# Rotary embedding on one core: the loads of slabs 5 to 7 and the stores of slabs 0 to 3 go in runs of 4 KB instead of 32 KB

## The chip, the cores and the metric

The kernel runs on one core of a Trainium2 chip. The metric is device time in microseconds (us), the median of several executions; lower is better. The profile is of one execution. Its engines are ScalarE (ACT), VectorE (DVE), GpSimd (POOL), TensorE (PE) and SyncE (SP), and there are 16 DMA engines that move data between HBM and SBUF for all queues.

## The reference

A rotary position embedding over x of 16 batches x 512 positions x 1024 values (float32, 33.55 MB), seen as 16 heads of 64. Within a head the two halves of 32 are turned by the angle of the position:

```python
x = x.reshape(batch, seq, num_heads, head_dim)
x1, x2 = x[..., :half_dim], x[..., half_dim:]
cos = cos[None, :, None, :]
sin = sin[None, :, None, :]
rotated = np.concatenate([x1 * cos - x2 * sin,
                          x1 * sin + x2 * cos], axis=-1)
```

cos and sin are 512 x 32 float32 tables (64 KB each). The output has the shape and type of x, so 33.55 MB are read and 33.55 MB written.

## The kernel before

**Tiling.** The 16 batches are worked through as 8 slabs of two batches each (`nb = 2`). A slab is 128 partitions x 8192 float32 values, so 32 KB in each partition and 4 MB in all. One partition holds 8 consecutive positions of 1024 values (`rpp = 8`), which are contiguous in HBM and in SBUF. `dram(t, s)` on L47 describes a slab in HBM as 128 rows of `W` = 8192 contiguous elements. A load or a store of a slab is one DMA of 128 runs of 32 KB, 8 runs for each of the 16 DMA engines.

**Slots.** Five slabs have room in SBUF (`slots = 5`). Slabs 0 to 4 are loaded at once at the start. Slab s + 5 takes the place of slab s, so `load(s + 5)` waits until the store of slab s has landed in HBM. The call stands behind the store in the program, on L143.

**Queues.** SyncE issues the loads of slabs 0 to 5 and the two small loads of cos and sin (which follow the load of slab 0). GpSimd issues the loads of slabs 6 and 7. ACT issues all eight stores, between its own compute instructions. On the profile's page q1 is SyncE's DMA queue, q10 is ACT's and q0 is GpSimd's.

**Tables.** POOL casts cos and sin to bf16, PE spreads them over the 128 partitions with a selection matrix, and DVE copies them to `tab` once. This is over before the first slab is worked on.

**Work on a slab.** A slab is worked on in passes: slabs 1 to 5 in one pass of 8192 elements per partition, slabs 0, 6 and 7 in two passes of 4096. For each pass ACT casts the float32 slab to bf16 (`xb`, L112), DVE does two multiplications (L133) and one addition (L136), and ACT casts the result back to float32 into the slab itself (L139). After the last pass of a slab ACT issues its store (L141). Two buffers `xb` alternate.

**Order.** The order on each engine is the program's order; nothing is planned at run time. ACT's order is: cast of the next pass, copy-out of this pass, then, if the slab is complete, its store. The cast of the first half of slab 7 therefore stands ahead of the copy-out of the second half of slab 6 and ahead of the store of slab 6. If slab 7 has not landed, ACT waits there.

## Time and profile before

| what | value |
|---|---|
| median of 3 runs | 162.8 us (162.47 to 166.78) |
| span of the profiled execution | 160.2 us |
| ACT busy | 113.5 us (71%), 23 instructions |
| DVE busy | 108.6 us (68%), 34 instructions |
| bytes moved by DMA | 67.24 MB, mean 420 GB/s |
| load of a slab from SyncE, issue to landing | 26.6 us (median) |
| load of a slab from GpSimd, issue to landing | 24.9 us (median) |
| store of a slab from ACT, issue to landing | 25.9 us (median) |

The profiled execution's own time is not given apart from its span, from its first to its last instruction. The median of the runs is 2.6 us above that span; this difference holds what lies around the instructions, and what one execution differs from another.

In the page, a row of digits cuts the span in 40 equal slices of 4 us; each digit is the busy share in tenths, 9 being 90% or more. A DMA queue's row has its packets, its megabytes, and the time that its packets took as a share of 16 engines. The shares of all queues together say how full the DMA engines were. A row of a group of instructions has the line, the engine, the operation, out <- in with the shapes and the count, then the total busy time, the mean of one in ns, and behind the last bar the idle time of the engine just before them with what ended it. A timeline row has the start and the duration in us. "ACTq", "SPq" and "POOL ... DMA_DIRECT2D" rows are issues of DMAs, not the transfers.

### The profile page before, as it was taken

Reading aid. Unit: us, or ns where it says so; the run is one execution under the profiler, and the core shown is the slowest. Engines: PE = TensorE matmul, PEld = TensorE weight load, DVE = VectorE, ACT = ScalarE, POOL = GpSimd, SP = SyncE. Lnnn points to the kernel's source line nnn. Section 1 sums busy time; section 2 is a strip of 40 time slices with the busy share of each in tenths; the row PEclk is TensorE's granted clock in tenths of the full one; section 3 lists DMA queues with packets and bytes.
Section 4 is the critical chain, followed back from the end, with each engine's and each line's share of the span. In section 5 each row is a group of like instructions: output and inputs, shape, how many; then the busy total and the mean of one; then the engine's idle time right before and its main releaser. Section 6 shows DMA issues by size and latency. Waiting matters only on the chain.

```text
span 160.2 us, 159 instructions
## 1 busy us (share of the span) xinstructions
PE 1.0 (1%) x4; PEld 0.5 (0%) x4; DVE 108.6 (68%) x34; ACT 113.5 (71%) x23; POOL 3.0 (2%) x11
## 2 busy tenths in 40 slices
PE   0002000000000000000000000000000000000000
PEld 0000000000000000000000000000000000000000
DVE  0001899999979979997997299919839499940000
ACT  3006929998999999899919995089995999553000
POOL 2001000000000000000010001000000000000000
DMA  7999999999999999999999999999999999999995
GB/s 246 409 393 426 393 450 466 393 417 491 401 393 426 491 393 409 499 401 393 483 434 393 450 466 393 426 483 401 409 491 409 393 475 442 393 442 475 393 426 229
DMA packets 2464, 67.24 MB, mean 420 GB/s; under 512 B 288, under 2 KB 416, under 8 KB 416
## 3 DMA queue, kind: packets, MB, share of 16 engines
q10 hardware_dynamic: 1152, 33.55, 48.5%
q1 hardware_dynamic: 1024, 25.30, 37.5%
q0 software_dynamic: 288, 8.39, 12.1%
HBM read 33.69 MB, written 33.55 MB: 420 GB/s over the span
## 4 chain that ended last, share of the span: by engine, by line
DMA 49%; ACT 28%; issue 8%; DVE 4%; SPq 1%; ACTq 0%; POOLq 0%
DMA slab<-in_x_dram 29%; DMA out_dram<-slab 20%; ACT slab L139 16%; ACT xb L112 12%; DVE xb L136 1%; DVE xb L133 1%; DVE slab L133 1%; SPq L73 1%; ACTq L141 0%; SPq L64 0%; POOLq L174 0%; ACTq L139 0%; POOLq L64 0%
## 5 line engine op out<-in xcount | busy, mean ns | idle before, releaser
L112 ACT CAST xb<-slab 128x4096 bf16<-128x4096 f32 (+1 forms) x11 | 56.6, 5155 | 27.8 <-DMA slab<-in_x_dram 26.5
L139 ACT CAST slab<-xb 128x4096 f32<-128x4096 bf16 (+1 forms) x11 | 56.6, 5154 | 3.5 <-DVE xb L136 3.5
L133 DVE TENSOR_TENSOR slab<-xb,tab 128x4096 bf16<-128x4096 bf16 (+1 forms) x11 | 35.9, 3260 | 17.3 <-ACT xb L112 17.2
L133 DVE TENSOR_TENSOR xb<-xb,tab 128x4096 bf16<-128x4096 bf16 (+1 forms) x11 | 35.9, 3261 | 0.3
L136 DVE TENSOR_TENSOR xb<-xb,slab 128x4096 bf16<-128x4096 bf16 (+1 forms) x11 | 35.9, 3261 | 0.3
L103 DVE CAST tab<-acc 128x1024 bf16<-128x1024 f32 x1 | 1.2, 1225 | 15.2 <-PE acc L97 15.2
L64 POOL DMA_DIRECT2D slab<-in_x_dram x2 | 1.2, 608 | 84.1 <-DMA out_dram<-slab 84.1
L112 ACT ACT_TABLE_LOAD x1 | 1.3, 1283 | 0.7 <-PEq L160 0.7
L97 PE MATMUL acc<-tab,pick 64*128 64x256 bf16 x4 | 1.0, 402 | 14.2 <-POOL tab L92 14.2
L92 POOL CAST tab<-cos_sb 64x256 bf16<-64x256 f32 x1 | 0.4, 389 | 12.1 <-DMA cos_sb<-in_cos_dram 12.1
L85 POOL TENSOR_SCALAR_AFFINE_SELECT pick<-pick 64x128 bf16<-64x128 bf16 x2 | 0.5, 285 | 0.1
L97 PEld LDWEIGHTS <-pick 64*128 64x128 bf16 x4 | 0.5, 122 | 14.2 <-issue 12.6
L92 POOL CAST tab<-sin_sb 64x256 bf16<-64x256 f32 x1 | 0.4, 394 | 0.0
L82 POOL MEMSET pick<- 64x256 bf16 x1 | 0.3, 304 | 0.3 <-POOLq L160 0.3
L160 POOL MEMSET const-float32-0.0<- 128x1 f32 x1 | 0.1, 103 | 0.2 <-issue 0.2
L160 POOL MEMSET const-bfloat16-1.0<- 128x1 bf16 x1 | 0.1, 107 | 0.0
L160 POOL MEMSET const-uint8-127<- 128x1 uint8 x1 | 0.1, 106 | 0.0
L160 POOL MEMSET const-float32-1.0<- 128x1 f32 x1 | 0.1, 103 | 0.0
## 6 DMA issues: line engine op xcount, KB each, us to landing
out_dram<-slab ACTq DMA_DIRECT2D x8, 4096.0 KB, 25.9
slab<-in_x_dram SPq DMA_DIRECT2D x6, 4096.0 KB, 26.6
slab<-in_x_dram POOLq DMA_DIRECT2D x2, 4096.0 KB, 24.9
cos_sb<-in_cos_dram SPq DMA_DIRECT2D x1, 64.0 KB, 12.5
sin_sb<-in_sin_dram SPq DMA_DIRECT2D x1, 64.0 KB, 12.3
```

The source lines that it names most:

```text
L64: queue.dma_start(out=slab[s], in_=dram(x, s))
L73: nc.sync.dma_start(out=t, in_=bass.AP(tensor=src.tensor, offset=src.offset, ap=[[TW, SP], [1, TW]]))
L82: nc.gpsimd.memset(pick, 0.0)
L85: nc.gpsimd.affine_select(out=part, in_=part, compare_op=mybir.AluOpType.not_equal, fill=1.0 - 2.0 * g, base=0, pattern=[[0, P // SP], [-1 ...
L92: nc.gpsimd.tensor_copy(out=view(tab1, i * TW, (1, TW)), in_=t)
L97: nc.tensor.matmul(view(acc, i * rpp * hd + h * half, (hd, rpp), (1, half)), view(pick, i * h * P, (1, P)), view(tab1, i * TW, (half, rpp) ...
L103: nc.vector.tensor_copy(out=tab, in_=acc)
L112: nc.scalar.copy(out=view(xb[s], r * dim, (1, n * dim)), in_=view(slab[s], r * dim, (1, n * dim)))
L133: nc.vector.tensor_mul(out=t, in0=xu, in1=view(tab, a + r * hd, (hd, n), (0, nh), (1, hd)))
L136: nc.vector.tensor_add(out=xu, in0=xu, in1=view(t2, half, (hd, n * nh), (-half, 2), (1, half)))
L139: nc.scalar.copy(out=xs, in_=xu)
L160: nc = _bacc.Bacc("TRN2", target_bir_lowering=False, num_devices=1)
```

## The change

A keyword `max_dma_last_dim` (in bytes) limits the length of one run of a DMA. With `4 * W` it is the whole row of a slab, 32 KB, as before; with `4 * dim` it is 4 KB, so that each of the 128 rows is cut in 8 runs and the DMA has 1024 runs.

- The loads of slabs 0 to 4 keep runs of 32 KB; those of slabs 5, 6 and 7 go in runs of 4 KB.
- The stores of slabs 0 to 3 go in runs of 4 KB; those of slabs 4 to 7 keep 32 KB.
- The loads of slabs 6 and 7 are issued by SyncE instead of GpSimd, so all loads are in SyncE's queue.

Compute, bytes, slots, waits and the order on ACT and DVE stay as they are.

```diff
     def load(s):
 
-        queue = nc.sync if s < nslabs - 2 else nc.gpsimd
         slab[s] = slabs.tile([P, W], f32, tag="slab", name="slab")
-        queue.dma_start(out=slab[s], in_=dram(x, s))
+        nc.sync.dma_start(out=slab[s], in_=dram(x, s),
+                          max_dma_last_dim=4 * (W if s < slots else dim))
 
...
 
         nc.scalar.copy(out=xs, in_=xu)
         if r + n == rpp:
-            nc.scalar.dma_start(out=dram(out_flat, s), in_=slab[s])
+            nc.scalar.dma_start(out=dram(out_flat, s), in_=slab[s],
+                                max_dma_last_dim=4 * (dim if s < 4 else W))
             if s + slots < nslabs:
                 load(s + slots)
```

## The prediction

> **What bounds the kernel now.** I read the page's second and third parts first, then the chain, then the groups, and last the DMA queues in short windows. From the page:

> ```profile
> DMA  7999999999999999999999999999999999999995
> DMA packets 2464, 67.24 MB, mean 420 GB/s; under 512 B 288, under 2 KB 416, under 8 KB 416
> q10 hardware_dynamic: 1152, 33.55, 48.5%
> q1 hardware_dynamic: 1024, 25.30, 37.5%
> q0 software_dynamic: 288, 8.39, 12.1%
> DMA 49%; ACT 28%; issue 8%; DVE 4%; SPq 1%; ACTq 0%; POOLq 0%
> L112 ACT CAST xb<-slab 128x4096 bf16<-128x4096 f32 (+1 forms) x11 | 56.6, 5155 | 27.8 <-DMA slab<-in_x_dram 26.5
> ```

> The DMA engines are busy in all 40 slices; the three queues' shares add to 98.1% of the span (157.2 of 160.2 us). ACT, the busiest compute engine, works 113.5 us and waits 26.5 us for loads. So the bytes are the bound: no reordering alone can gain more than the 3.0 us in which the engines are not all busy, and of those 1.7 us precede the first packet and 1.2 us follow the last. The packet records give 1213 ns for a 32 KB packet in the mixed stages, started every 1209.5 ns, so one slab is 8 x 1.2095 = 9.68 us of every engine.

> How do loads and stores share the engines? Three windows of 1.2 us, one packet time each, show it. The columns of a queue row are packets, MB and share of 16 engines. First 65.0 to 66.2 us:

> ```profile
> q1 hardware_dynamic: 16, 0.52, 101.1%
> ```

> Then 66.2 to 67.4 us:

> ```profile
> q10 hardware_dynamic: 16, 0.52, 101.1%
> ```

> Then 67.4 to 68.6 us:

> ```profile
> q1 hardware_dynamic: 16, 0.52, 101.1%
> ```

> Each window holds 16 packets, one per engine, of one queue only: SyncE's loads (q1), ACT's stores (q10), loads again. **The queues take turns of one 32 KB packet.** Equal halves of the bandwidth are thus a consequence of equal packets. The change makes the packets unequal.

> The end hangs on slab 7. From the timeline:

> ```profile
> 99.23 0.53 POOL L64 DMA_DIRECT2D slab<-in_x_dram  x1 [18.65 <-DMA out_dram<-slab]
> ...
> 124.22 3.60 ACT L112 CAST xb<-slab 128x4096 bf16<-128x4096 f32 x1 [1.85 <-DMA slab<-in_x_dram]
> ...
> 131.37 0.34 ACTq L141 DMA_DIRECT2D out_dram<-slab  x1
> ...
> 145.54 0.34 ACTq L141 DMA_DIRECT2D out_dram<-slab  x1
> ```

> Load 7 lands at T = 124.22. ACT takes its first half ahead of slab 6's second copy-out (program order), so store 6 is issued at T + 7.15 and store 7 at T + 21.32. Store 6's last packets end at 149.1, so store 7, issued at 145.54, finds the engines still fed: a margin of 3.6 us, less about 1.0 us from an issue to a first packet (slab 0: issued at 0.74, first packet at 1.74).

> **The parts of the change.**

> *Descriptor overhead.* Seven of the sixteen transfers (stores 0 to 3, loads 5 to 7) go in 4 KB packets: 64 instead of 8 per engine and slab. No 4 KB packet is in the trace; bound it by the 1 KB packets of cos and sin (46 ns long, started 42 ns apart) and the 32 KB ones. A line through the starts gives 155 ns for 4 KB, through the durations 159 ns. Eight of them are 1240 to 1272 ns against 1210 or 1213: 30 to 59 ns more per 32 KB. With 7 x 8 = 56 such runs per engine that is 1.7 to 3.3 us of pure engine time, nothing beside which it could hide. Below zero is excluded, since a 32 KB packet already runs at 27.0 GB/s per engine and smaller ones only add starts. I take 156 ns, near the starts (they are what a queue can deliver): 9.98 us per slab, +2.2 us in all.

> *Issue.* One ACT issue of 128 rows took 338 ns, SyncE's 328 to 585, the 64-row cos and sin 522 and 583: no growth with rows is seen. If it grew with packets, 8 x 338 = 2.7 us, so 2.4 us more on ACT for each of four stores, 9.5 us before its cast of slab 5 at 84.2. Its waits there (3.54 us at 84.2, 6.69 at 104.8) swallow that. I take zero. If ACT were even held at each issue until the store before had drained, store 4 would be issued near 113 and store 5 near 124, still before step 4 below needs them.

> *SyncE instead of GpSimd for loads 6 and 7.* It removes two GpSimd issues (0.69 and 0.53 us) and puts two behind load 5 on SyncE, which has nothing else to do by then. Load 7 already started only behind load 6. Worth: zero.

> *Turns of unequal length.* This decides. Step by step, T of load 7 after the change:

> 1. Loads 3 and 4 (32 KB) beat store 0 (4 KB) 8 to 1 and land earlier. ACT is busy then (22.8 of 23.6 us from 37.6 to 61.2), so nothing is won. Loads 0 to 4 and store 0 together were served by 62.0 us; with 8 x 0.04 us more, store 0's data now ends at 62.3.
> 2. Load 5 waits for its landing. Before, it was 0.45 us to the issue and 4.4 us (61.21 to 65.6) to the first packet, two queued 32 KB packets (2.4 us) among it. Two 4 KB packets instead are 0.3 us: store 1 has the engines alone for 2.7 us (bounds 1.5, from slab 0's 1.0 us, and 4.8, as before).
> 3. Then loads 5, 6, 7 and stores 1, 2, 3 alternate, 4 KB each, and the stores stay 2.7 us of service ahead. Store 3 ends at 62.3 + 2.7 + 2 x (3 x 9.98 - 2.7) = 119.5. Load 7 was issued at about 100, behind load 6, and has 2.7 / 0.156 = 17 packets per engine left.
> 4. From here ACT's queue holds stores 4 and 5 (issued near 98 and 116) in 32 KB packets. A turn of both queues costs 1.21 + 0.156 = 1.366 us and moves one 4 KB packet of load 7. Before, the same turn moved 32 KB. Stores 4 and 5 have 16 packets, so 16 turns, 21.9 us, to 141.4; the last packet and 0.45 us to the landing: **T = 141.9**.
> 5. Store 6 can't be issued until T + 7.15 = 149.1. Queue and engines are empty from 141.5, which is new idle time.
> 6. The end: T + 21.3 (store 7's issue) + 1.2 (first packet) + 9.7 (its 8 packets alone) + 1.2 (last packet to the span's end, as now) = T + 33.4 = **175.3 us** of span.

> The page has only the span of the profiled execution, 160.2 us; the median of the runs, 162.8, is 2.6 above it. Adding this gives 177.9 us, +9%. The 2.2 us of overhead are inside this sum, not on top.

> Bounds: with a lead of 1.5 us store 3 ends at 120.7 and 10 packets are left, 13.7 us, T = 134.8, time 170.8. With any lead of 2.5 or more, stores 4 and 5 run out and T stays near 142. With 159 ns packets, store 3 ends 1.1 us later: 179.

> [...]

> The windows above show turns of a single descriptor, for 32 KB ones; whether small ones are grouped no row shows.

> **Rivals.**

> 1. *Turns go by bytes, several 4 KB packets in a row* (the not-slower side). With n per turn, the 17 left need 17/n turns of 1.21 + 0.156 n. The engines then stay fed to 160.2 + 2.2 = 162.4 if T is below 129.0, that is if the rest takes under 9 us: n = 3 or more decides for it. Time 162.8 + 2.2 = 165.0 (164.5 to 166.1), inside 2%, which is also about what a measurement of this kernel can tell from no change. For: equal halves now. Against: strict single turns now.
> 2. *Two per turn:* 8.5 turns of 1.52, 12.9 us, T = 132.9, time 168.9.
> 3. *The split is undone on the way to the queues:* packets stay at 32 KB, only the move to SyncE is left. 162.8.
> 4. *Loads 3 and 4 come early, ACT gets ahead:* even with all 12 us of ACT's later waits for loads gone (3.5, 6.7 and 1.9 us), the engines' 157.2 us stay, and with them some 162 us at best; the overhead takes more than that gain.
> 5. *A 4 KB packet costs far more than the line says*, as switching after each one is not free: at 180 ns a slab takes 11.5 us, store 3 ends 10 us later, and the time is about 187. Nothing in the rows above speaks for it: turns of 32 KB start without a gap.

> **How the numbers follow.** Forecast 0.69; rival 1 0.12; rival 2 0.11; rival 3 0.03; rival 4 0.02; rival 5 0.03. The range takes in the forecast's bounds (170.8 to 179) and rival 2 (168.9): 167 to 180, 0.80 of the chance. Faster by over 2% would need more than the 3.0 us in which the engines are not all busy, with no overhead: 0.01, out of rival 4. Within 2%: rivals 1 and 3 and the rest of 4, 0.16. Slower: forecast, rivals 2 and 5, 0.83.

> **What would show it.** In the page of the changed kernel: q10 and q1 with some 4,700 and 4,000 packets (eight for each split row, and 16 small ones per transfer for the semaphores) and no q0 (steps on packets); load 4 landing in the mid-fifties; in a window from 120 to 140, a q1 row with about 16 packets of 4 KB per engine against 16 of 32 KB on q10; the cast of slab 7 waiting some 18 us at L112; a hole in the DMA row near slices 36 to 37; store 7 issued near 163. If L112 waits for slab 7 only to about 126, turns are not single packets and I am wrong; if ACTq L141 rows last microseconds, the issue term is wrong.

## The result and the profile after

The changed kernel takes **176.88 us** (median of 4 runs, 176.80 to 177.06) against 162.65 us for the kernel before: a ratio of **1.089, 95% interval 1.087 to 1.092**. The forecast was 177.9 us. The profiled execution took 176.92 us with a span of 175.1 us, so here 1.8 us lie around the span. (Some executions of the kernels that move most slabs in 32 KB take some 3 to 6 us more than the others, the kernel before among them; the ratios leave these out, so a median below and its ratio may differ.)

The page of the changed kernel, the lines that answer to those shown of before (DMA row in 40 slices of 4.4 us, packets, queues, chain, ACT's casts of the slabs):

```profile
DMA  7998989999998999999999999999999920892695
DMA packets 8736, 67.24 MB, mean 384 GB/s; under 512 B 288, under 2 KB 416, under 8 KB 7584
q1 hardware_dynamic: 4000, 33.69, 46.2%
q10 hardware_dynamic: 4736, 33.55, 45.6%
DMA 55%; ACT 25%; issue 7%; DVE 4%; SPq 1%; ACTq 0%
L112 ACT CAST xb<-slab 128x4096 bf16<-128x4096 f32 (+1 forms) x11 | 56.6, 5155 | 45.3 <-DMA slab<-in_x_dram 43.9
```

The change does what it says: q0 is gone, and the packet counts are those of seven slabs cut in eight. ACT's busy time in its casts is 56.6 us as before; what grew is its idle time ahead of them, 26.5 to 43.9 us waiting for loads. Near the end the DMA row, full throughout before, has a hole (2, 0) and a second dip (2). The timeline says where the wait is:

```profile
87.52 7.02 ACT L112 CAST xb<-slab 128x8192 bf16<-128x8192 f32 x1 [6.55 <-DMA slab<-in_x_dram]
...
141.73 3.60 ACT L112 CAST xb<-slab 128x4096 bf16<-128x4096 f32 x1 [16.77 <-DMA slab<-in_x_dram]
...
148.87 0.34 ACTq L141 DMA_DIRECT2D out_dram<-slab  x1
...
163.05 0.34 ACTq L141 DMA_DIRECT2D out_dram<-slab  x1
```

Load 7 lands at 141.73, 17.5 us later than before (124.22), and stores 6 and 7 are issued 7.1 and 21.3 us after it, as before. The DMA queues from 116.7 to 138.7 us, in which stores 4 and 5 and load 7 compete (packets, MB, share of 16 engines):

```profile
q10 hardware_dynamic: 281, 8.27, 87.0%
q1 hardware_dynamic: 283, 1.16, 12.8%
```

A packet of these rows is one run of a transfer, on one of the 16 engines (159 ns for 4 KB, 1213 ns for 32 KB), or one of the 16 packets of 4 bytes at a transfer's end (288 for the 18 transfers, 9 ns each). The two queues moved the same number of packets (283 and 281), and the stores seven times the bytes (seven and not eight, since 27 of q10's packets are such small ones; only with them are the counts equal). So in this window one packet was one turn, at 4 bytes, 4 KB and 32 KB alike.

### The profile page after: what moved, and what is told of

Read it like the earlier page. It is cut to its first block, busy times and chain, and to the rows that moved or that the text cites. A ratio compares the mean times of both kernels' runs of the same rounds, so it can differ in the third digit from the quotient of the medians.

```text
span 175.1 us, 157 instructions
## 1 busy us (share of the span) xinstructions
PE 1.0 (1%) x4; PEld 0.5 (0%) x4; DVE 108.6 (62%) x34; ACT 113.5 (65%) x23; POOL 1.8 (1%) x9
## 2 busy tenths in 40 slices
DMA packets 8736, 67.24 MB, mean 384 GB/s; under 512 B 288, under 2 KB 416, under 8 KB 7584
## 3 DMA queue, kind: packets, MB, share of 16 engines
q10 hardware_dynamic: 4736, 33.55, 45.6%
HBM read 33.69 MB, written 33.55 MB: 384 GB/s over the span
## 4 chain that ended last, share of the span: by engine, by line
DMA 55%; ACT 25%; issue 7%; DVE 4%; SPq 1%; ACTq 0%
DMA slab<-in_x_dram 37%; DMA out_dram<-slab 18%; ACT slab L139 14%; ACT xb L112 11%; DVE xb L136 1%; DVE xb L133 1%; DVE slab L133 1%; SPq L73 1%; ACTq L141 0%; SPq L63 0%; ACTq L139 0%
## 5 line engine op out<-in xcount | busy, mean ns | idle before, releaser
L112 ACT CAST xb<-slab 128x4096 bf16<-128x4096 f32 (+1 forms) x11 | 56.6, 5155 | 45.3 <-DMA slab<-in_x_dram 43.9
L139 ACT CAST slab<-xb 128x4096 f32<-128x4096 bf16 (+1 forms) x11 | 56.6, 5153 | 3.5 <-DVE xb L136 3.5
L97 PEld LDWEIGHTS <-pick 64*128 64x128 bf16 x4 | 0.5, 122 | 14.4 <-issue 12.8
```

The source lines that it names most:

```text
L97: nc.tensor.matmul(view(acc, i * rpp * hd + h * half, (hd, rpp), (1, half)), view(pick, i * h * P, (1, P)), view(tab1, i * TW, (half, rpp) ...
L112: nc.scalar.copy(out=view(xb[s], r * dim, (1, n * dim)), in_=view(slab[s], r * dim, (1, n * dim)))
L139: nc.scalar.copy(out=xs, in_=xu)
```

## The experiments

All edits are to the changed kernel; ratios are to the kernel before. The theory is the forecast's step 4: queues take turns of one packet, so load 7 in 4 KB packets is starved by stores 4 and 5 in 32 KB packets. The rivals of this section have numbers of their own, apart from the prediction's: (1) 4 KB packets are slow wherever they are; (2) the loss comes from putting all loads in one queue; (3) slabs that land early save time. Each text under an edit is what was expected before the run.

### Load 7 in 32 KB again

```diff
-                          max_dma_last_dim=4 * (W if s < slots else dim))
+                          max_dma_last_dim=4 * (dim if s in (5, 6) else W))
```

> As the changed kernel, but load 7 goes in runs of 32 KB again. Theory (queues take turns of one packet, and load 7 in 4 KB packets is starved by the 32 KB packets of stores 4 and 5): load 7 lands near 117 us of the span, ACT never waits 10 us at L112 late in the kernel, the engines stay fed, and only the overhead of six slabs in 4 KB packets is left, 6 x 0.26 = 1.6 us: 164 to 165 us. Rival 1 (4 KB packets are slow wherever they are, 14.2 us over seven slabs): 176.9 - 2.0 = 174.9 us. Rival 2 (all loads in SyncE's one queue): 177 us.

Measured: **163.51 us, ratio 1.008 (1.005 to 1.010)**, a little under the 164 to 165 expected. One slab of the seven gives back 13.4 of the 14.2 us. ACT has no wait for slab 7 at all; the line of its first cast of slab 7 has no idle time before it:

```profile
124.90 3.60 ACT L112 CAST xb<-slab 128x4096 bf16<-128x4096 f32 x1
```

Rival 1 and rival 2 fall: six slabs still go in 4 KB packets, and all loads are still in one queue.

### Stores 4 and 5 in 4 KB too

```diff
-                                max_dma_last_dim=4 * (dim if s < 4 else W))
+                                max_dma_last_dim=4 * (dim if s < 6 else W))
```

> As the changed kernel, but stores 4 and 5 go in runs of 4 KB too; load 7 keeps its 4 KB. Theory: it is the length of the competitor's packet that starves load 7, so with equal packets load 7 lands near 128 us and the time is the fill plus nine slabs of overhead, 9 x 0.26 = 2.4 us: 164.5 to 167 us. Rival 1 (4 KB packets are slow in themselves): two more slabs of them, 176.9 + 4.1 = 181 us. Rival 2 (one queue for the loads): 177 us.

Measured: **164.38 us, ratio 1.012 (1.008 to 1.016)**. This keeps load 7 as it is and changes only what it competes with; there are more small packets than in the changed kernel, and 12.5 us less time. The queues of this run from 117 to 126 us and, in its timeline, ACT's cast of slab 7:

```profile
q1 hardware_dynamic: 465, 1.90, 51.3%
q10 hardware_dynamic: 465, 1.89, 51.0%
```

```profile
127.56 3.60 ACT L112 CAST xb<-slab 128x4096 bf16<-128x4096 f32 x1 [2.37 <-DMA slab<-in_x_dram]
```

With equal packets the bytes were equal (1.90 and 1.89 MB), and load 7 lands at 127.56, within the 129.0 that the prediction's rival 1 gave as the point where nothing is lost.

### SyncE's queue alone

```diff
-                          max_dma_last_dim=4 * (W if s < slots else dim))
+                          max_dma_last_dim=4 * W)
...
-                                max_dma_last_dim=4 * (dim if s < 4 else W))
+                                max_dma_last_dim=4 * W)
```

Only the move of loads 6 and 7 from GpSimd to SyncE is left.

> The kernel before with loads 6 and 7 issued by SyncE, all packets 32 KB. Theory: nothing, 162.7 us, ratio 0.995 to 1.01. Rival 2 (load 7 waits in one queue behind load 6 instead of taking its own turns): most of the 14 us, 170 to 177 us.

Measured: median 166.61 us, **ratio 0.999 (0.996 to 1.003)**; the profiled execution took 162.72 us. The move costs nothing.

### Load 7 alone in 4 KB

```diff
-                          max_dma_last_dim=4 * (W if s < slots else dim))
+                          max_dma_last_dim=4 * (dim if s == 7 else W))
...
-                                max_dma_last_dim=4 * (dim if s < 4 else W))
+                                max_dma_last_dim=4 * W)
```

> As the run with all packets of 32 KB and all loads on SyncE, but load 7 alone in runs of 4 KB: one slab of the seven. Theory: from 103 us, when load 6 is through, stores 3, 4 and 5 have 22 packets of 32 KB left, 22 turns of 1.365 us to 133 us, in which load 7 moves 22 of its 64 packets; the other 42 take 6.5 us alone; landing at 140 us, the span 173.5 and the time 175 to 176.5 us, nearly the whole loss from one slab. Rival 1 (each slab in 4 KB packets costs 2.0 us): 164.7 us.

Measured: median 176.00 us, **ratio 1.084 (1.074 to 1.094)**; the profiled execution took 175.33 us with a span of 173.6. The timeline of this run:

```profile
140.15 3.60 ACT L112 CAST xb<-slab 128x4096 bf16<-128x4096 f32 x1 [19.12 <-DMA slab<-in_x_dram]
```

One slab of sixteen makes nearly the whole loss, and load 7 lands where the count of turns put it (140).

### All slabs in 4 KB

```diff
-                          max_dma_last_dim=4 * (W if s < slots else dim))
+                          max_dma_last_dim=4 * dim)
...
-                                max_dma_last_dim=4 * (dim if s < 4 else W))
+                                max_dma_last_dim=4 * dim)
```

> All sixteen slab transfers in runs of 4 KB. Theory: the queues are equal again, load 7 lands near 128 us, and what is left is the overhead of sixteen slabs, 16 x 0.26 = 4.2 us: 166.5 to 168 us. Rival 1 (each slab in 4 KB packets costs 2.0 us): 162.7 + 32 = 195 us.

Measured: **167.11 us, ratio 1.027 (1.024 to 1.031)**. Against the run with SyncE's queue alone the span grows from 160.9 to 165.3 us: 4.4 us for sixteen slabs, 0.28 us each. That is the price of small packets as such; the changed kernel has seven of them, 1.9 us of its 14.2.

### Stores 0 to 3 alone in 4 KB

```diff
-                          max_dma_last_dim=4 * (W if s < slots else dim))
+                          max_dma_last_dim=4 * W)
```

> Only stores 0 to 3 in runs of 4 KB, all loads 32 KB on SyncE. Theory: the loads win the engines, land earlier, and nothing is gained by it, since the engines were full; four slabs of overhead, 4 x 0.26 = 1.0 us: 163.5 to 164.5 us. Rival 3 (slabs that come early let ACT get ahead and save its waits): below 161 us. Rival 1: 162.7 + 8.1 = 171 us.

Measured: **163.82 us, ratio 1.007 (1.003 to 1.010)**. Here the loads win against the stores. The queues of this run from 67.5 to 77.5 us, with load 5 in 32 KB packets beside store 1 in 4 KB packets:

```profile
q1 hardware_dynamic: 112, 3.67, 87.4%
q10 hardware_dynamic: 112, 0.46, 11.1%
```

This is the mirror image of the changed kernel: the same number of packets, and now the load has eight times the bytes. So in these two windows it was the packet's length that decided, and neither the queue nor the direction: the side in 32 KB packets had 87.0% of the engines as a store and 87.4% as a load. ACT never waits for slab 7, yet nothing is won: the engines were full already (98.1% of the span before). Rival 3 falls.

### Loads 5 to 7 alone in 4 KB

```diff
-                                max_dma_last_dim=4 * (dim if s < 4 else W))
+                                max_dma_last_dim=4 * W)
```

> Only loads 5 to 7 in runs of 4 KB, all stores 32 KB. Theory: load 5 is starved too, by stores 1, 2 and 3: 21 of its 64 packets per engine move until store 3 is through near 94 us, the rest then alone, so it lands near 101 us instead of 84; ACT waits some 16 us there, stores 4 and 5 come late, load 6 and most of load 7 have the engines alone, load 7 lands near 131 us, and ACT's chain, not load 7, sets the end: span 169, time 169 to 174 us. Rival 1 (2.0 us for each slab in 4 KB packets): 168.8 us, with load 5 landing at 85 us.

Measured: median 173.82 us, **ratio 1.055 (1.049 to 1.062)**; the profiled execution took 171.32 us with a span of 169.5 (expected 169). The timeline:

```profile
84.23 14.26 SPq L63 DMA_DIRECT2D slab<-in_x_dram  x1
...
101.61 7.02 ACT L112 CAST xb<-slab 128x8192 bf16<-128x8192 f32 x1 [20.84 <-DMA slab<-in_x_dram]
```

The starving moves to load 5, which lands at 101.6 instead of 84.2 us. This half of the change alone costs less than both together: since ACT waits earlier, store 4 is issued only at 115.58 and store 5 at 129.09, and by the packet records load 7 has the engines alone from 110.9 us until store 4's first packet at 119.1; its last data ends at 131.2. The first line, an issue of 14.26 us, is taken up at the end.

### 16 KB in the place of 4 KB

```diff
-                          max_dma_last_dim=4 * (W if s < slots else dim))
+                          max_dma_last_dim=4 * (W if s < slots else 4 * dim))
...
-                                max_dma_last_dim=4 * (dim if s < 4 else W))
+                                max_dma_last_dim=4 * (4 * dim if s < 4 else W))
```

> As the changed kernel with 16 KB in the place of 4 KB. Theory: a turn of both queues costs 1.21 + 0.61 = 1.82 us and moves 16 KB of load 7; store 3 ends near 115 us with 9 such packets of load 7 left, 16.4 us, so it lands near 132 us, the span is 165.5 and the time 167 to 168 us: between the two kernels, since the share follows the packet's length. If turns went by bytes: 163 us. Rival 1 (overhead per packet alone, a quarter of the packets): 162.7 + 14.2 / 4 = 166 us, but without a wait of ACT for slab 7.

Measured: **165.64 us, ratio 1.019 (1.015 to 1.023)**, below the expected 167 to 168. The timeline of this run:

```profile
130.47 3.60 ACT L112 CAST xb<-slab 128x4096 bf16<-128x4096 f32 x1 [6.72 <-DMA slab<-in_x_dram]
```

The mechanism is there (a wait of 6.72 us for slab 7), the size was off: load 7 had some 8 packets per engine left when store 3 ended, not 9, and landed at 130.5 instead of 132; adding the 33.4 us of the prediction's step 6 to 130.5 gives 163.9, which is the span. This is 1.6 us under the expected span of 165.5 and most of the miss. By its time alone (165.64 us) this run does not part the theory from rival 1's 166 us; the wait for slab 7, which that rival excludes, does.

### Slab 6's store ahead of ACT's wait for slab 7

The forecast's steps 5 and 6 leave open what the cost is: engines that idle because store 6 comes late, or the landing of load 7 itself. The first try moved the cast of slab 7's first half behind the store in the program:

```diff
-        if i + 1 < len(passes):
+        late = i + 1 < len(passes) and passes[i + 1][:2] == (nslabs - 1, 0)
+        if i + 1 < len(passes) and not late:
             cast(passes[i + 1])
...
             if s + slots < nslabs:
                 load(s + slots)
+        if late:
+            cast(passes[i + 1])
```

> As the changed kernel, but ACT casts the first half of slab 7 only after the store of slab 6 has been issued, so store 6 no longer waits for load 7. Theory: store 6 is issued near 132 us and gives the stores' queue eight more 32 KB packets to take turns with: 24 turns from 116.5 to 149.3 us, load 7 has 10 packets left then and lands near 151.5 us, store 7 is issued 21 us later, the span is 184.5 and the time 186 us: an earlier store makes it slower. Rival (the loss is that store 6 comes late, for ACT's order, and the engines idle): load 7 lands at 141 us as before, the idle time after it is filled, the time 177 us or less.

Measured: **176.91 us, ratio 1.087 (1.084 to 1.091)**, the same as the changed kernel, and not the 186 us expected. The timeline of this run:

```profile
128.42 3.60 ACT L140 CAST slab<-xb 128x4096 f32<-128x4096 bf16 x1 [3.56 <-DVE xb L137]
141.76 3.60 ACT L112 CAST xb<-slab 128x4096 bf16<-128x4096 f32 x1 [9.73 <-DMA slab<-in_x_dram]
141.76 0.34 ACTq L142 DMA_DIRECT2D out_dram<-slab  x1
...
162.92 0.34 ACTq L142 DMA_DIRECT2D out_dram<-slab  x1
```

The edit did not do what it was meant to. The copy-out that store 6 needs ended at 132.0, but ACT's built instruction order still has the cast of slab 7 ahead of the store, so the store was issued at 141.76, only 7.1 us earlier than in the changed kernel. (In this run the order on ACT was thus that of the built program, and not that of the program's lines, as the part on the kernel before has it.) Still it says something: seven microseconds earlier for store 6 are worth nothing, because store 7 is issued 21.2 us after load 7's landing all the same.

The second try keeps this edit and also stores slab 6 in two halves, each after its own copy-out; both are then issued ahead of the cast:

```diff
+        if s == nslabs - 2:
+            nc.scalar.dma_start(out=dram(out_flat, s, r * dim, n * dim), in_=xs)
-        if r + n == rpp:
+        elif r + n == rpp:
```

> As the changed kernel, but store 6 is issued near 132 us, as two stores of one half each (runs of 16 KB, 8 packets per engine each), ahead of ACT's cast of slab 7; so the stores' queue does not run dry at 139 us. Theory: load 7 has 15 packets per engine left when store 5 is through at 138.7 us, and each now costs a turn of 0.61 + 0.155 us; load 7 lands near 150.5 us instead of 141.7, store 7 is issued 21.2 us after that, the span is 183.5 and the time 184 to 187 us: stores issued earlier make it slower. Rival (the loss is the idle engines after 141 us, because store 6 comes late): load 7 lands near 142 us, the idle time is filled, 177 us or less.

Measured: **185.61 us, ratio 1.143 (1.137 to 1.150)**. The timeline of this run:

```profile
128.68 3.95 ACTq L142 DMA_DIRECT2D out_dram<-slab  x2
151.10 7.11 ACT L112 CAST xb<-slab 128x4096 bf16<-128x4096 f32 x2 [18.84 <-DMA slab<-in_x_dram]
...
172.01 0.34 ACTq L144 DMA_DIRECT2D out_dram<-slab  x1
```

Stores issued at 128.7 and 132.3, while load 7 was still in flight, moved its landing from 141.7 to 151.1 us and the whole kernel back by as much (the span by 9.1 us). Two stages of it, below the same stretch of the changed kernel (stretch, length, busy time of PE, PEld, DVE, ACT and POOL, clock, share of the DMA engines, GB/s):

```profile
138.70:151.00 12.30, 0.00 (x0) 0.00 (x0) 5.56 (x3) 9.27 (x3) 0.00 (x0) 1.00 0.35 145
```

```profile
138.70:151.00 12.30, 0.00 (x0) 0.00 (x0) 0.00 (x0) 0.00 (x0) 0.00 (x0) 1.00 0.97 413
151.00:172.00 21.00, 0.00 (x0) 0.00 (x0) 13.48 (x6) 14.32 (x4) 0.00 (x0) 1.00 0.00 0
```

The stretch in which the changed kernel's engines mostly stood idle is filled, and in its place they stand idle from load 7's landing until store 7. By the packet records the idle time in all grew from 12.6 us (8.4 ahead of store 6, 4.3 ahead of store 7) to 21.7. So the idle time is not there because store 6 comes late. In every run in which the engines ran empty near the end (the changed kernel, load 7 alone in 4 KB, 16 KB, and both tries here) the span ends 33.1 to 33.5 us after load 7's landing. What cost the time in these runs is the last load's landing.

### All slabs in 8 KB

```diff
-                          max_dma_last_dim=4 * (W if s < slots else dim))
+                          max_dma_last_dim=4 * 2 * dim)
...
-                                max_dma_last_dim=4 * (dim if s < 4 else W))
+                                max_dma_last_dim=4 * 2 * dim)
```

> All sixteen slab transfers in runs of 8 KB. Queues equal, so no starving: overhead of 16 slabs, by a line through the packet starts of 4 and 32 KB some 0.11 us each, 1.8 us in all: 164 to 165 us. On the issue: with all packets 4 KB SyncE's issues of loads 2, 3 and 4 took 7.5, 10.2 and 10.0 us and ended when 84 to 89 earlier packets per engine were left. If a queue takes a new DMA only below some 85 packets, then here load 2 (74 before it) is issued in under 1 us, load 3 (107) is held until about 9 to 10 us of the span, and load 4 until about 16 to 18 us. If the hold goes by the number of DMAs or by bytes, load 2 is held as it was there, or none is held.

Measured: **164.35 us, ratio 1.013 (1.009 to 1.017)**; SyncE's issues took 0.70 us for load 2, 6.7 us for load 3 (until 10.5 us of the span) and 9.3 us for load 4 (until 19.9). The last ends later than the 16 to 18 us expected; the two others go as a limit on packets has it, and load 2, held for 7.5 us in 4 KB packets, is no longer held. The time is that of equal queues with a small overhead: 162.5 us of span against 160.9.

## Why the prediction was right, step by step

**What bounds the kernel, and that the engines take turns of one packet:** right, and shown for unequal packets: 281 and 283 packets in the same 22 us, 112 and 112 in the run with the stores alone, and in the 16 KB run, with packets of 16 KB beside 32 KB, a landing (130.5) between those of the two kernels (124.22 and 141.73). In the two windows with equal counts a turn was a single packet, also at 4 KB. The prediction's rivals 1 and 2, several packets per turn, fall by these counts; rival 3 falls by the packet counts of the page, rival 4 by the run with the stores alone, rival 5 by the 159 ns packets.

**Descriptor overhead (156 ns, 2.2 us in all):** right. The 4 KB packets are 159 ns long and started every 155.3 ns; 0.28 us per slab by the run with all slabs in 4 KB, so 1.9 us for seven.

**Issue and SyncE's queue at zero:** right for this kernel. ACT's issues of 1024 packets took 378 to 428 ns instead of 338 to 377. The hold that I bounded does exist (below), but not in the changed kernel. The move to SyncE measured 0.999.

**Step 1, loads 0 to 4 and store 0:** right. Load 4 landed at 54.1 and store 0 at 62.3.

**Step 2, the lead of store 1 (2.7 us): wrong.** Load 5 was issued at 62.74 and its first packets came at 66.9 to 67.2, 4.2 to 4.5 us later, no sooner than before. I had put 2.4 of the 4.4 us down to two 32 KB packets queued ahead; with 4 KB packets there it did not shrink. The 4.4 us of before were no measure of this either: load 4's last data ran there until 63.2 us, 2.0 us after load 5's issue, so the queue was not yet empty. The lead was about 5.1 us, beyond the 4.8 of my bounds.

**Step 3, store 3's end (119.5) and 17 packets left: wrong in size, following from step 2.** Store 3 ended at 116.4 to 117.3 and load 7 had some 32 packets per engine left.

**Step 4, T = 141.9: right (141.73), and not by luck alone.** Sixteen turns from 116.7 to 138.7 us are the 21.9 us forecast. The doubled rest did not show because the bound that the prediction named held: with any lead of 2.5 us or more, stores 4 and 5 run out first and load 7 is the last of fourteen transfers. Its landing is then the time in which the engines move fourteen slabs, whatever the order within. What remained of load 7 (some 14 packets per engine) went alone from about 139 to 141 us. So T is blind to steps 2 and 3, and its agreement confirms neither. With 32 packets left, even two per turn (16 turns of rival 2's 1.52 us from 116.7) would have ended near 141; the single turns are shown by the packet counts and not by T.

**Steps 5 and 6:** right in numbers: store 6 at 148.87 (149.1), store 7 at 163.05, span 175.1 (175.3). The 14.9 us by which the span grew are 12.6 us of new idle time and some 2 us of overhead. But the half-slab run shows what step 5 leaves open: the idle time does not come from store 6 being late; it follows from load 7's landing, and grows with it. The 17.5 us that load 7 is late become 14.9 us of span, because before, store 7 found the engines still fed and had slack (issued at 145.54, with store 6's packets running until 149.3).

**From span to time:** I added 2.6 us; 1.8 would have been right, which is most of the 1.0 us between 177.9 and 176.88.

## What to carry to other kernels

Where two DMA queues competed in this kernel, the length of a packet set the share of the bandwidth: a transfer in 4 KB packets got about one eighth of the engines beside one in 32 KB packets (12.8 against 87.0%), and a half beside one of its own kind (51.3 against 51.0%). So before cutting a transfer's rows, ask what will stand in the other queue at that time, and do not give the last load, on which the tail of the compute hangs, shorter packets than the stores it meets: here that was 13.4 of the 14.2 us. In this kernel, which fills its DMA engines, earlier landings in the middle gained nothing (ratio 1.007 with the stores alone), and the idle stretches near the end were the trace of a late landing: bringing store 6 forward did not shorten them (12.5 and 21.7 us in the two tries, for 12.6).

## What was not expected of the hardware

```profile
95.36 4.18 ACTq L141 DMA_DIRECT2D out_dram<-slab  x1
```

By the packet records, each of these ended when 78 to 89 packets per engine of the earlier transfers of its queue were left, with 4 KB and 8 KB packets alike and the small ones counted, and issues with 71 to 78 ahead of them were not held. So in these runs the hold went by packets, not by transfers or bytes: load 2 took 7.5 us to issue in 4 KB packets and 0.70 us in 8 KB packets, with the same transfers and the same bytes ahead of it. In the run with the stores alone the held issue stood ahead of ACT's next cast, which began at 99.57, behind the issue's end (99.54). A wait hid nearly all of it: load 6, which that cast needs, had its last packets at 98.6 us.

**In these runs the first packet of a transfer on an empty queue came 3.4 to 5.1 us after its issue while the engines were busy, and 0.8 to 1.0 us after it when they were idle** (stores 6 and 7 after). By the packet records of the 16 engines, the busy cases are store 0 beside the loads' 32 KB packets (3.4 to 5.1 us before, 3.7 to 4.6 after), load 5 after, beside 4 KB packets (4.2 to 4.5), and store 0 in the run with all slabs in 4 KB (3.6 to 4.0). My reading put 2.4 us of it down to two queued 32 KB packets; beside 4 KB packets these would be 0.3 us, and the delay is as long there, so the reading is wrong. What sets the delay was not tried and stays open.
